# A second-layer triangular solution traced in three parts behind two chunk states, and the gated outputs' store moved from ScalarE's queue to GpSimd's

## The chip, the cores and the metric

The kernel runs on one core of one Trainium2 chip. The core has five engines that work beside each other, each through its own list of instructions and in order: TensorE (PE, matrix products, with its weight load PEld), VectorE (DVE), ScalarE (ACT), GpSimd (POOL) and SyncE (SP, which here only issues DMA transfers). They wait for each other by semaphores. Transfers are issued from the queues of SP, ACT and POOL. The metric is the time of one execution in microseconds (us) on the device.

## The reference

Two residual layers work on 512 tokens of width 2048. The first is differential attention, which the change does not touch. The second is RWKV-7 time mixing: 32 heads of 64 channels carry a matrix state S over the tokens.

```
def step(S, inp):
    r_t, w_t, k_t, v_t, a_t, b_t = inp
    sa = jnp.einsum('bhvk,bhk->bhv', S, a_t)
    S = S * w_t[:, :, None, :] + sa[..., None] * b_t[:, :, None, :] + v_t[..., None] * k_t[:, :, None, :]
    y = jnp.einsum('bhvk,bhk->bhv', S, r_t)
    return S, y
...
y = (y - mean) * lax.rsqrt(var + GN_EPS)            # per head, then gain, bias and a bonus term
y = y.reshape(B, T, RW_WIDTH).astype(h.dtype) * jax.nn.silu(g)
return y @ w_out, v_first
```

r, k, v and the gate g come from one projection of the normalised input, mixed with the token before; w, a and b come from two narrow projections and k.

## The kernel before

**Tiles.** The second layer (`layer1`) goes over 16 pairs of heads (128 channels). The loop variable is j; one pass is called a round here. A pair's 512 tokens are cut into 8 chunks of 64. Within a chunk the recurrence is a triangular system, so that only the state between chunks is sequential.

**A round** runs four projections on PE, `pp` in the profile (L122): v of pair j, k of pair j+1, the gate of pair j-2, r of pair j+1. Each has 16 blocks of 128 rows times three products (high and low halves of fp32 numbers), in two halves. The weights come by SP in 512 KB loads (`wraw`, L78), ACT makes the high half (`wh`, L105), DVE the low half (`wl`, L106), which frees the `wraw` buffer for the next load.

**The chain of a pair** (`t_combine`, `scan_pair`) is threaded between the projection's matmuls one round later: pair j-1 in round j. For each chunk c, PE makes `sm` from the state `VS` and the tile `G` (L1490), ACT copies `rhs` (L1493), PE multiplies by the solution `TT` (L1501), ACT copies the result into `VS` (L1503), PE makes the next state's sum (L1508), and DVE writes the state of chunk c+1 in two halves (L1512, L1515 for the first). "The state of chunk 5" is the one that is written after the step of chunk 4. Between two products stand 6 or 8 projection matmuls. At the end PE makes the outputs `Y` (L1530, L1534), DVE centres them (L1545 to L1547).

**The solution** (`t_solve`) inverts the triangular blocks of pair j in round j, on DVE: 31 steps i, each a product into `tmpl` (L1374) and an addition into `Tm` (L1376). Step i has a row of 31-i columns and i//4+1 blocks, which is how a step is known in the profile (128x66 is step 20). Then comes a multiply (L1377), and SP stores `Tm` into DRAM as `td` (L1378). At the next chain's start SP reads it back in four loads (`TT`, L1391); DVE transposes their first blocks (`T`, L1401, one instruction for each head), PE makes `px` from T and G (L1407), ACT copies it to `X` (L1410), PE makes `px` from TT and X (L1418). In between, the same stretch makes the next pair's Gram products `gp` (L1317), which need `AR` (DVE, L1290). ACT's cast `sHx` of `mixr` (L1112), which is DVE's next product (L1291), stands ahead of the copy X on ACT.

**The gate's output** (`gated`): `mixv` is the gate (`gate`: tanh on ACT, L1455; product on DVE, L1456), times `y` (L1461). ACT's queue stores it into the DRAM tensor yd2 (`yd`, L1464), from where the out projection reads it much later.

**What sets the order.** The program is traced in one order of Python calls; a scheduler then orders each engine's list when the kernel is built, by priority and by its own estimate of when inputs are ready. `high_priority(offset=...)` moves a piece ahead: the projections' splits by 2000 (`AHEAD`), the chain by 3000 (`SCAN`), the solution by 4000 (`SOLVE`). `issue_after(x)` keeps a piece behind instruction x. A chain's step is also allowed to run small pieces (`others`) once a chunk.

Of the kernel before, what the change touches and what calls it, by code (L numbers as in the profile page):

```python
# [18 lines left out]
ALU = mybir.AluOpType  # L19
# [4 lines left out]
P = 128  # L24
D = 2048
# [13 lines left out]
AHEAD, SCAN, SOLVE = 2000, 3000, 4000  # L39


def ahead(offset):


    def deco(f):
        def g_(g, *a, **k):
            with g.tc.high_priority(offset=offset):
                return f(g, *a, **k)

        return g_  # L50

    return deco
# [1055 lines left out]
def split_act(g, src, pool, tag):  # L1108
    nc = g.nc
    hh = pool.tile(list(src.shape), F32R, name="sH" + tag, tag=tag + "H", bufs=1)  # L1110
    hl = pool.tile(list(src.shape), F32R, name="sL" + tag, tag=tag + "L", bufs=1)
    nc.scalar.copy(hh[:], src)  # L1112
    nc.vector.tensor_sub(hl[:], src, hh[:].bitcast(F32))
    return hh, hl
# [35 lines left out]
HALF = 32  # L1150
NG = 4
# [54 lines left out]
LAG = 2  # L1206
# [76 lines left out]
def stage2(g, j, r, p):  # L1283

    nc = g.nc
    while g.later:
        g.later.pop(0)[1]()
    col = lambda n: g.prm[n][:, j : j + 1]
    with g.tc.high_priority(offset=2 * SOLVE if 0 < j <= LAG else 0):
        nc.vector.tensor_mul(p.AR[:, :, 1, :], r[:].rearrange("p (c t) -> p c t", c=NC_), p.E[:, :, 1:])  # L1290
    nc.vector.scalar_tensor_tensor(r[:], r[:], col("hrk"), p.f[:], ALU.mult, ALU.mult)  # L1291
    p.rf = r
# [51 lines left out]
def turn_keys(g, p, c0):  # L1344

    nc = g.nc
    ps = g.ps.tile([P, 512], F32, name="pt", tag="pb", bufs=2)
    for i in range(4):
        nc.tensor.transpose(ps[:, i * P : (i + 1) * P], p.BK[:, c0 + i].rearrange("p s t -> p (s t)"), g.ident[:])
    nc.scalar.copy(p.BKT[:, c0 : c0 + 4], ps[:].rearrange("p (c k) -> p c k", c=4))  # L1350


@ahead(SOLVE)
def t_solve(g, j, p):


    nc, w = g.nc, g.work
    NQ = HALF // NG
    LT = w.tile([P, HALF + 1, HALF], F32, name="LT", tag="LT", bufs=1)
    Tm = w.tile([P, NQ, HALF], F32, name="Tm", tag="Tm", bufs=1)  # L1360
    tmp = w.tile([P, NQ * HALF], F32, name="tmpl", tag="tmpl", bufs=1)
    for i in range(NG):
        ld = nc.gpsimd.dma_start(out=LT[i * 32 : i * 32 + 32], in_=g.ltd[j % 2].rearrange("b h c s t -> (b h c) s t"))
    n2 = LT[:, HALF, :]
    nc.vector.tensor_scalar(n2, n2, 1e-24, None, ALU.max)
    nc.vector.reciprocal(n2, n2)
    nc.gpsimd.memset(Tm[:], 0.0)
    tf = Tm[:].rearrange("p q t -> p (q t)")
    for i in range(NG):
        nc.gpsimd.memset(tf[i * 32 : i * 32 + 32, i :: HALF + NG], 1.0)  # L1370
    for i in range(HALF - 1):
        n, s = HALF - 1 - i, i // NG + 1
        tt = tmp[:, : n * s].rearrange("p (a b) -> p a b", a=s)
        nc.vector.scalar_tensor_tensor(tt, LT[:, i : i + 1, i + 1 :].to_broadcast([P, s, n]), n2[:, i : i + 1],  # L1374
                                       Tm[:, 0:s, i : i + 1].to_broadcast([P, s, n]), ALU.mult, ALU.mult)
        nc.vector.tensor_add(Tm[:, 0:s, i + 1 :], Tm[:, 0:s, i + 1 :], tt)  # L1376
    nc.vector.tensor_mul(Tm[:], Tm[:], n2[:, None, :].to_broadcast([P, NQ, HALF]))  # L1377
    nc.sync.dma_start(out=g.td[j % 2].rearrange("q l t -> l q t"), in_=Tm[:])  # L1378
    return ld.ins


GAP_D, GAP_X, GAP_T = 18, 10, 8


def t_combine(g, j, p, lead):
# [52 lines left out]
def turn_values(g, p):  # L1438

    nc, w, v = g.nc, g.work, p.v  # L1440
    p.VS = w.tile([P, NC_, 2, C], F32, name="VS", tag="VS", bufs=2)
    ps = g.ps.tile([P, 512], F32, name="pt", tag="pd", bufs=1)
    for t in range(NT):
        nc.tensor.transpose(ps[:, t * P : (t + 1) * P], v[:, t * P : (t + 1) * P], g.ident[:])
    pv = ps[:].rearrange("p (t h n) -> p t h n", t=NT, h=2)
    for h in range(2):
        for par in range(2):
            nc.scalar.copy(p.VS[(1 - h) * C : (2 - h) * C, par : NC_ : 2, h, :], pv[par * C : par * C + C, :, h, :])
# [11 lines left out]
def gated(g, j, p, gt, last=False):  # L1460
    g.nc.vector.tensor_mul(gt[:], gt[:], p.y[:])  # L1461
    if last:
        return
    g.nc.scalar.dma_start(out=g.yd2[j * P : (j + 1) * P, :], in_=gt[:])  # L1464


HEADS = ((0, slice(0, C)), (1, slice(C, P)))
# [2 lines left out]
def chain(g, j, p, delay, gap, gap_s, others=(), lead=GAP_D - GAP_T):  # L1470
    def steps():
        yield from t_combine(g, j, p, lead)
        yield from scan_pair(g, j, p, gap, gap_s, dict(others))

    p.chain = Chain(g, steps(), delay)
    return p.chain
# [74 lines left out]
def group_norm(g, j, p):  # L1551
    p.chain.finish(g)
    nc, w, yc = g.nc, g.work, p.yc
    NG = 2 * NT
    sq = w.tile([P, NG, C], F32, name="ysq", tag="ysq", bufs=1)
    nc.scalar.activation(sq[:], yc[:], AF.Square)
    var = g.small.tile([P, NG], F32, name="var", tag="var", bufs=3)
    nc.vector.reduce_sum(var[:], sq[:], AX.X)
    nc.vector.tensor_scalar(var[:], var[:], 1.0 / C, GN_EPS, ALU.mult, ALU.add)
    rs = g.small.tile([P, NG], F32, name="rsg", tag="rsg", bufs=3)  # L1560
    rsqrt(g, rs[:], var[:], NG, "r8")
    nc.vector.tensor_mul(yc[:], yc[:], rs[:, :, None].to_broadcast([P, NG, C]))


def finish_y(g, j, p, bank=("pd", 1)):
    nc, yc = g.nc, p.yc
    ps = g.ps.tile([P, 512], F32, name="pt", tag=bank[0], bufs=bank[1])
    for t in range(NT):
        nc.tensor.transpose(ps[:, t * P : (t + 1) * P], yc[:, 2 * t : 2 * t + 2, :].rearrange("p h n -> p (h n)"),
                            g.ident[:])  # L1570
    nc.vector.scalar_tensor_tensor(p.y[:], ps[:], g.prm["hgw"][:, j : j + 1], p.y[:], ALU.mult, ALU.add)


def layer1(g, aps):
    nc, tc = g.nc, g.tc
    with ExitStack() as cx:
# [6 lines left out]
        def proj(i, j, **k):  # L1583
            return unit_chan(g, (aps["rw_w_in"], i * KT + j), P, **k)[0]
# [17 lines left out]
        for j in range(D // P):  # L1602
            p = pairs[j]
            if j:
                others = [(0, lambda p=p: turn_keys(g, p, 0)), (1, lambda p=p: turn_keys(g, p, 4)),
                          (2, lambda p=p: turn_values(g, p))]
                if j > LAG + 1:
                    others[0] = (0, lambda p=p, i=j - 2: (turn_keys(g, p, 0), finish_y(g, i, pairs[i])))
                elif j > 1:
                    others.append((3, lambda i=j - 2: finish_y(g, i, pairs[i])))  # L1610
                full = LAG < j < D // P - 1
                gaps = ((6, 8) if j > LAG + 1 else (5, 6)) if full else (4, 4) if j > LAG else (4, 5)
                leads = {1: 64, LAG: 18, LAG + 1: 42}
                chain(g, j - 1, pairs[j - 1], 5, *gaps, others, leads.get(j, GAP_D - GAP_T)).step(g)
            stage2(g, j, r, p)
            normed = j > LAG + 1 and pairs[j - 2].chain.wait is None
            if normed:
                group_norm(g, j - 2, pairs[j - 2])

            def behind(m, j=j, p=p, normed=normed):  # L1620
                if j > 1:
                    pairs[j - 2].chain.finish(g)
                with tc.issue_after(m.ins):
                    gram(g, j, p, j > LAG + 1 and pairs[j - 1].chain)
                p.rfs = split_act(g, p.rf[:], w, "x")
                mask_gram(g, p, 0)
                loaded = t_solve(g, j, p)
                with tc.issue_after(loaded):
                    mask_gram(g, p, 1)
                if j > 1 and not normed:  # L1630
                    group_norm(g, j - 2, pairs[j - 2])

            stage_v(g, j, p, proj(2, j, behind=(18, behind)))
            if j == 0:
                turn_keys(g, p, 0)
                turn_keys(g, p, 4)
                turn_values(g, p)
            if j == 1:
                first = gate_of(0, "g0")
            if j + 1 < D // P:  # L1640
                begin(j + 1)
            if j > LAG:
                gated(g, j - LAG, pairs[j - LAG], gate_of(j - LAG))
            if j + 1 < D // P:
                r = receptances(j + 1)
            if j == LAG:
                gated(g, 0, pairs[0], first)
# [52 lines left out]
        for nm in ("11", "21", "22", "12"):  # L1700
            t, c = PLACES[nm]
            a = w.tile([P, 2, 512], F32, name="acc", tag="AR", bufs=3)
# [86 lines left out]
```

## Time and profile before

| | |
|---|---|
| three runs | 2084.47, 2084.9, 2086.21 us (median 2084.9) |
| the profiled execution | 2085.74 us, its span 2084.0 |
| PE busy | 2056.8 us, 99% of the span |
| DVE busy | 1605.5 us, 77% |
| ACT busy | 1124.6 us, 54% |
| POOL busy | 392.4 us, 19% |
| granted TensorE clock | 1.000 |

Names in the profile are `out<-in`, L is the line of the code, x the count. A `q` behind an engine (SPq, ACTq) is its queue issuing a transfer. In a timeline the first number is the start and the second the length in us; what stands in brackets is the idle time of the engine before it and what ended it. Matmul ends are modelled, so the distance between two starts says more about PE than the lengths. The rows of one steady round, shown below from about 1350 to 1421 us, stand for all of rounds 4 to 14.

### The profile page before, as it was taken

Reading aid. Unit: us, or ns where it says so; the run is one execution under the profiler, and the core shown is the slowest. Engines: PE = TensorE matmul, PEld = TensorE weight load, DVE = VectorE, ACT = ScalarE, POOL = GpSimd, SP = SyncE. Lnnn points to the kernel's source line nnn. Section 1 sums busy time; section 2 is a strip of 40 time slices with the busy share of each in tenths; the row PEclk is TensorE's granted clock in tenths of the full one; section 3 lists DMA queues with packets and bytes.
Section 4 is the critical chain, followed back from the end, with each engine's and each line's share of the span. In section 5 each row is a group of like instructions: output and inputs, shape, how many; then the busy total and the mean of one; then the engine's idle time right before and its main releaser. Section 6 shows DMA issues by size and latency. Waiting matters only on the chain.

```text
span 2084.0 us, 34169 instructions
## 1 busy us (share of the span) xinstructions
PE 2056.8 (99%) x11948; PEld 1675.6 (80%) x11948; DVE 1605.5 (77%) x4113; ACT 1124.6 (54%) x2238; POOL 392.4 (19%) x751
## 2 busy tenths in 40 slices
PE   9999999999999999999999999999999999999999
PEld 7888888888888888878777787888888778877887
DVE  6988988888898976475778878777777887767645
ACT  5765656556665544355465555555555555545322
POOL 1020211102011000101222332232332222232001
PEclk9999999999999999999999999999999999999999
DMA  8487978879788966723333332323333233346565
GB/s 271 143 175 192 179 173 184 164 190 166 188 180 169 273 214 172 167 78 111 97 81 92 92 96 85 96 79 100 99 95 90 84 94 91 101 135 189 185 162 121
DMA packets 159549, 294.61 MB, mean 141 GB/s; under 512 B 64416, under 2 KB 81824, under 8 KB 159376
## 3 DMA queue, kind: packets, MB, share of 16 engines
q1 hardware_dynamic: 110912, 184.91, 28.8%
q0 software_dynamic: 23808, 83.54, 22.2%
q10 hardware_dynamic: 24656, 23.97, 3.6%
q8 instruction: 94, 1.54, 0.3%
q14 instruction: 79, 0.65, 0.1%
HBM read 268.71 MB, written 23.66 MB: 140 GB/s over the span
## 4 chain that ended last, share of the span: by engine, by line
PE 75%; DVE 17%; ACT 3%; issue 3%; DMA 2%; ACTq 0%; DVEq 0%; SPq 0%
PE pp L122 35%; PE pp L573 21%; PE pt L122 5%; DVE tmpl L1374 3%; DVE wl L106 3%; DVE Tm L1376 2%; PE gp L1317 1%; PE sc L122 1%; PE sm L1490 1%; ACT wh L105 1%; PE o L122 1%; DVE VS L1512 1%; PE lora L122 1%; PE z L122 1%; PE sm L1501 1%
## 5 line engine op out<-in xcount | busy, mean ns | idle before, releaser
L106 DVE TENSOR_TENSOR wl<-wraw,wh 128x1024 fp32r<-128x1024 f32 (+2 forms) x291 | 356.4, 1225 | 210.8 <-ACT wh L105 202.4
L105 ACT CAST wh<-wraw 128x1024 fp32r<-128x1024 f32 (+2 forms) x291 | 303.6, 1043 | 266.2 <-PE pp L122 133.1
L122 PE MATMUL pp<-hL,wh 128*128 128x512 f32 x1024 | 414.2, 404 | 0.0
L122 PE MATMUL pp<-hH,wh 128*128 128x512 f32 x1024 | 413.2, 404 | 0.0
L122 PE MATMUL pp<-hH,wl 128*128 128x512 f32 x1024 | 412.9, 403 | 0.0
L122 PEld LDWEIGHTS pp<-hH,wh 128*128 128x128 f32 x1024 | 193.2, 189 | 34.5 <-issue 0.2
L122 PEld LDWEIGHTS pp<-hL,wh 128*128 128x128 f32 x1024 | 193.2, 189 | 33.4
L122 PEld LDWEIGHTS pp<-hH,wl 128*128 128x128 f32 x1024 | 193.4, 189 | 32.5
L573 PE MATMUL pp<-wh,hH 128*128 128x512 f32 x448 | 177.0, 395 | 0.0
L573 PE MATMUL pp<-wh,hL 128*128 128x512 f32 x448 | 175.8, 393 | 0.0
L1496 POOL COPY SA<-VS 64x64 f32<-64x64 f32 x224 | 74.4, 332 | 415.9 <-DVE VS L1512 380.1
L122 PE MATMUL pp<-wh,hH 128*128 128x512 f32 x372 | 145.9, 393 | 2.4 <-ACT hH L1103 2.4
L122 PE MATMUL pp<-wh,hL 128*128 128x512 f32 x372 | 146.5, 394 | 0.1
L122 PE MATMUL pp<-wl,hH 128*128 128x512 f32 x372 | 145.9, 392 | 0.5 <-DVE wl L106 0.5
L1374 DVE SCALAR_TENSOR_TENSOR tmpl<-LT,Tm 128x60 f32<-128x60 f32 (+24 forms) x496 | 134.0, 270 | 12.3
L573 PE MATMUL pp<-wl,hH 128*128 128x512 f32 x448 | 140.4, 392 | 0.0
L1376 DVE TENSOR_TENSOR Tm<-Tm,tmpl 128x60 f32<-128x60 f32 (+24 forms) x496 | 104.2, 210 | 11.9
L1493 ACT COPY rhs<-sm 64x64 f32<-64x64 f32 x256 | 52.8, 206 | 105.9 <-PE sm L1490 86.1
L573 PEld LDWEIGHTS pp<-wl,hH 128*128 128x128 f32 x448 | 84.5, 189 | 17.2
L573 PEld LDWEIGHTS pp<-wh,hH 128*128 128x128 f32 x448 | 84.2, 188 | 17.3 <-issue 0.3
L573 PEld LDWEIGHTS pp<-wh,hL 128*128 128x128 f32 x448 | 84.3, 188 | 16.1
L1503 ACT COPY VS<-sm 64x64 f32<-64x64 f32 x256 | 52.7, 206 | 77.9 <-PE sm L1501 70.3
(400 smaller groups left out, 4367.4 us busy)
## 6 DMA issues: line engine op xcount, KB each, us to landing
wraw<-in_rw_w_in_dram SPq DMA_DIRECT2D x128, 512.0 KB
wraw<-in_da_w_in_dram SPq DMA_DIRECT2D x75, 512.0 KB
wraw<-in_da_w_in_dram POOLq DMA_DIRECT2D x28, 512.0 KB, 6.5
wraw<-in_da_w_out_dram SPq DMA_DIRECT2D x26, 512.0 KB
wraw<-in_rw_w_out_dram SPq DMA_DIRECT2D x26, 512.0 KB
Ta<-in_da_w_in_dram POOLq DMA_DIRECT2D x21, 512.0 KB, 5.8
Tb<-in_da_w_in_dram POOLq DMA_DIRECT2D x21, 512.0 KB, 5.8
Tc<-in_da_w_in_dram POOLq DMA_DIRECT2D x21, 512.0 KB, 5.8
```

What stands on the lines that cost most here:

```text
L105: a = nc.scalar.copy(hi[:, ks], raw[:, ks])
L106: d = nc.vector.tensor_sub(lo[:, ks], raw[:, ks], hi[:, ks].bitcast(F32))
L122: m = nc.tensor.matmul(out, a, b, start=s, stop=e, skip_group_check=skip)
L573: m = nc.tensor.matmul(out[t][:], x, wt[lo][:, k, :], start=first, stop=end and lo == 1 and k == KG - 1, skip_group_check=True)
L1317: m = nc.tensor.matmul(gp[h][:, i * P : (i + 1) * P], BK[r_, c0 + i, :, :], p.AR[r_, c0 + i, :, :], start=True, stop=True)
L1374: nc.vector.scalar_tensor_tensor(tt, LT[:, i : i + 1, i + 1 :].to_broadcast([P, s, n]), n2[:, i : i + 1], Tm[:, 0:s, i : i + 1].to_broadca ...
L1376: nc.vector.tensor_add(Tm[:, 0:s, i + 1 :], Tm[:, 0:s, i + 1 :], tt)
L1490: nc.tensor.matmul(sm[:, 0:P], both(p.G[:, c, 0]), both(VS[:, c]), start=True, stop=True)
L1493: nc.scalar.copy(rhs[r_, :], sm[r_, h * C : h * C + C])
L1496: nc.gpsimd.tensor_copy(p.SA[r_, c - 1, :], VS[r_, c, h, :])
L1501: nc.tensor.matmul(sm[:, P : P + C], both(g.TT[j % 2][:, c]), rhs[:], start=True, stop=True)
L1503: g.copied = nc.scalar.copy(VS[r_, c, h, :], sm[r_, P : P + C])
```

## The change

The solution's steps become a generator in three parts: steps 0 to 20, 21 to 28, and 29 to 30 with the multiply and the store `td`. In rounds 3 to 14 (`full`) the first part is traced where the whole was; the second is traced by the chain of the pair before, in its step of chunk 4, behind the instruction that writes the state of chunk 5, and the third in its step of chunk 6, behind the state of chunk 7. In the other rounds the solution stays in one piece. Apart from that, `gated` issues its store from POOL's queue instead of ACT's. No instruction is added or removed; 14 stores change queues.

```
-    for i in range(HALF - 1):
-        ...
-    nc.vector.tensor_mul(Tm[:], Tm[:], n2[:, None, :].to_broadcast([P, NQ, HALF]))
-    nc.sync.dma_start(out=g.td[j % 2].rearrange("q l t -> l q t"), in_=Tm[:])
+    def steps(a, b):
+        for i in range(a, b):
+            ...
+    def parts():
+        for a, b in zip(PARTS, PARTS[1:]):
+            with g.tc.high_priority(offset=SOLVE), g.tc.issue_after(g.state.ins) if a and split else ExitStack():
+                steps(a, b)
+                if b == HALF - 1:
+                    nc.vector.tensor_mul(Tm[:], Tm[:], n2[:, None, :].to_broadcast([P, NQ, HALF]))
+                    nc.sync.dma_start(out=g.td[j % 2].rearrange("q l t -> l q t"), in_=Tm[:])
+            if split:
+                yield
+    p.solve = parts()
+    next(p.solve, None)
...
+PARTS = 0, 21, 29, HALF - 1
...
-    g.nc.scalar.dma_start(out=g.yd2[j * P : (j + 1) * P, :], in_=gt[:])
+    g.nc.gpsimd.dma_start(out=g.yd2[j * P : (j + 1) * P, :], in_=gt[:])
...
+                if full:
+                    others += [(c, lambda p=p: next(p.solve)) for c in (4, 6)]
...
-                loaded = t_solve(g, j, p)
+                loaded = t_solve(g, j, p, LAG < j < D // P - 1)
```

The order of the lists moves as follows (in the changed kernel lines behind the edit have numbers 14 higher, L1512 is L1526, and L1374, L1376, L1377 and L1378 are L1376, L1378, L1385 and L1386).

DVE around the state of chunk 5 (`VS`), before:

```order
L1374 SCALAR_TENSOR_TENSOR tmpl<-LT,Tm 128x66
L1376 TENSOR_TENSOR Tm<-Tm,tmpl 128x6x11
L1374 SCALAR_TENSOR_TENSOR tmpl<-LT,Tm 128x60
L1376 TENSOR_TENSOR Tm<-Tm,tmpl 128x6x10
L1374 SCALAR_TENSOR_TENSOR tmpl<-LT,Tm 128x54
L1512 SCALAR_TENSOR_TENSOR VS<-sm,gam,Sg 64x64
```

and in the changed kernel:

```order
L1376 SCALAR_TENSOR_TENSOR tmpl<-LT,Tm 128x66
L1378 TENSOR_TENSOR Tm<-Tm,tmpl 128x6x11
L1526 SCALAR_TENSOR_TENSOR VS<-sm,gam,Sg 64x64 x2
L1376 SCALAR_TENSOR_TENSOR tmpl<-LT,Tm 128x60
L1263 TENSOR_TENSOR f<-f,mixk 128x512
```

The state's two halves stand three rows of the solution earlier, right behind step 20.

DVE around the state of chunk 7, before (mixv is the gate, sLup a split of two narrow weights that SP loads into a `wraw` buffer):

```order
L1374 SCALAR_TENSOR_TENSOR tmpl<-LT,Tm 128x16
L1144 SCALAR_TENSOR_TENSOR mixv<-pp,mu,mixv 128x511
L1376 TENSOR_TENSOR Tm<-Tm,tmpl 128x8x2
L1374 SCALAR_TENSOR_TENSOR tmpl<-LT,Tm 128x8
L1376 TENSOR_TENSOR Tm<-Tm,tmpl 128x8
L1377 TENSOR_TENSOR Tm<-Tm,LT 128x256
L1512 SCALAR_TENSOR_TENSOR VS<-sm,gam,Sg 64x64 x2
L1456 SCALAR_TENSOR_TENSOR mixv<-thg,mixv 128x512
L1461 TENSOR_TENSOR mixv<-mixv,y 128x512
L1113 TENSOR_TENSOR sLup<-upw,sHup 96x256
L106 TENSOR_TENSOR wl<-wraw,wh 128x1024
```

and in the changed kernel:

```order
L1470 SCALAR_TENSOR_TENSOR mixv<-thg,mixv 128x512
L1526 SCALAR_TENSOR_TENSOR VS<-sm,gam,Sg 64x64 x2
L1376 SCALAR_TENSOR_TENSOR tmpl<-LT,Tm 128x16
L1475 TENSOR_TENSOR mixv<-mixv,y 128x512
L1378 TENSOR_TENSOR Tm<-Tm,tmpl 128x8x2
L1113 TENSOR_TENSOR sLup<-upw,sHup 96x256
L1376 SCALAR_TENSOR_TENSOR tmpl<-LT,Tm 128x8
L1378 TENSOR_TENSOR Tm<-Tm,tmpl 128x8
L1385 TENSOR_TENSOR Tm<-Tm,LT 128x256
L106 TENSOR_TENSOR wl<-wraw,wh 128x1024
```

The last two steps and the multiply went behind the state and are mixed with the gate's second product and the split; the gate's first product went ahead of the state.

SP from the narrow weights (`upw`) on, before:

```order
L1589 DMA upw<-in_rw_decay_up_dram 96x128
L1590 DMA upw<-in_rw_iclr_up_dram 96x128
L1378 DMA td<-Tm 128x8x32
L78 DMA wraw<-in_rw_w_in_dram 128x1024
L1391 DMA TT_9512<-td 32x8x32 x4
L78 DMA wraw<-in_rw_w_in_dram 128x1024 x2
```

and in the changed kernel:

```order
L1603 DMA upw<-in_rw_decay_up_dram 96x128
L1604 DMA upw<-in_rw_iclr_up_dram 96x128
L78 DMA wraw<-in_rw_w_in_dram 128x1024
L1386 DMA td<-Tm 128x8x32
L78 DMA wraw<-in_rw_w_in_dram 128x1024
L1405 DMA TT_9512<-td 32x8x32 x4
L78 DMA wraw<-in_rw_w_in_dram 128x1024
```

One load of weights went ahead of td, so that td and TT each stand behind one now. The same holds from round 4 to round 13; round 14 has weights only between td and TT. On DVE the second transpose T (L1401) went three to five rows behind the first, among small operations of the group norm, and two of those went behind the split that follows. PE's list keeps its order but for a few places in rounds 3 and 4, ACT's steady rounds lose only the store, and on POOL the store stands behind the last copy of a chain's state, ahead of memsets.

More of the change, by code (lines that the diff above doesn't have):

```diff
@@ L1353, in t_solve @@
 @ahead(SOLVE)
-def t_solve(g, j, p):
+def t_solve(g, j, p, split):
     nc, w = g.nc, g.work
@@ L1370, in t_solve @@
         nc.gpsimd.memset(tf[i * 32 : i * 32 + 32, i :: HALF + NG], 1.0)
-    for i in range(HALF - 1):
[L1372 to L1378, printed above, removed]
+    def steps(a, b):
+        for i in range(a, b):
+            n, s = HALF - 1 - i, i // NG + 1
+            tt = tmp[:, : n * s].rearrange("p (a b) -> p a b", a=s)
+            nc.vector.scalar_tensor_tensor(tt, LT[:, i : i + 1, i + 1 :].to_broadcast([P, s, n]), n2[:, i : i + 1],
+                                           Tm[:, 0:s, i : i + 1].to_broadcast([P, s, n]), ALU.mult, ALU.mult)
+            nc.vector.tensor_add(Tm[:, 0:s, i + 1 :], Tm[:, 0:s, i + 1 :], tt)
+    def parts():
[9 more added lines that the diff above has]
+    next(p.solve, None)
     return ld.ins
 GAP_D, GAP_X, GAP_T = 18, 10, 8
+PARTS = 0, 21, 29, HALF - 1
 def t_combine(g, j, p, lead):
```

## The prediction

> **What bounds it now.** I read three views: the windows of one round of the second layer (a pass of the pair loop; rounds 4 to 14 are alike), the waits of TensorE (PE) over those rounds, and the timeline of one round.
>
> ```profile
> 1208.00:1268.30 60.30, 59.59 (x428) 48.65 (x427) 46.70 (x131) 32.90 (x75) 16.93 (x37) 1.00 0.32 94
> ```
>
> The columns are the stretch, its length, the busy time of PE, its weight loads, DVE, ACT and POOL, the granted clock, DMA share and GB/s. PE is busy for 59.59 of 60.30 us at full clock. So a round can only win back PE's few stops. Over rounds 4 to 14 (1208 to 1850 us) these are all of PE's waits (total us, times, longest):
>
> ```profile
> core 0 of [0], span 2084.0 us
> PE sm L1490 <- DVE VS L1512: 4.6, 12, 0.4
> PE sm L1501 <- ACT rhs L1493: 3.6, 11, 0.3
> ```
>
> Two waits, about once a round each. The timeline of PE in one round prices them:
>
> ```profile
> 1392.82 0.39 PE L122 MATMUL pp<-hL,wh 128*128 128x512 f32 x1
> 1393.05 0.39 PE L122 MATMUL pp<-hH,wl 128*128 128x512 f32 x1
> 1393.81 0.46 PE L1490 MATMUL sm<-VS,G 128*128 128x128 f32 x2 [0.38 <-DVE VS L1512]
> ...
> 1404.71 0.42 PE L1490 MATMUL sm<-VS,G 128*128 128x128 f32 x2
> ...
> 1406.13 0.40 PE L122 MATMUL pp<-hH,wh 128*128 128x512 f32 x1
> 1406.85 0.43 PE L1501 MATMUL sm<-rhs,TT 128*128 128x64 f32 x2 [0.33 <-ACT rhs L1493]
> ```
>
> A projection matmul gives way to the next after 0.23 us (1392.82 to 1393.05). The product on the state of chunk 5 starts 0.76 us after its forerunner: 0.53 lost. The one on rhs of chunk 7 starts 0.72 us after: 0.49 lost. Both together, 1.02 us a round, are what this change can win there. Now who causes them, on DVE and ACT:
>
> ```profile
> 1392.95 0.27 DVE L1512 SCALAR_TENSOR_TENSOR VS<-sm,gam,Sg 64x64 f32<-64x64 f32 x1
> ...
> 1403.12 0.23 DVE L1374 SCALAR_TENSOR_TENSOR tmpl<-LT,Tm 128x8 f32<-128x8 f32 x1
> 1403.38 0.17 DVE L1376 TENSOR_TENSOR Tm<-Tm,tmpl 128x8 f32<-128x8 f32 x1
> 1403.59 0.43 DVE L1377 TENSOR_TENSOR Tm<-Tm,LT 128x256 f32<-128x256 f32 x1
> 1403.93 0.60 DVE L1512 SCALAR_TENSOR_TENSOR VS<-sm,gam,Sg 64x64 f32<-64x64 f32 x2
> 1404.56 0.69 DVE L1456 SCALAR_TENSOR_TENSOR mixv<-thg,mixv 128x512 f32<-128x512 f32 x1
> 1405.28 0.69 DVE L1461 TENSOR_TENSOR mixv<-mixv,y 128x512 f32<-128x512 f32 x1
> 1405.89 0.41 DVE L1113 TENSOR_TENSOR sLup<-upw,sHup 96x256 fp32r<-96x256 f32 x1
> ```
>
> ```profile
> 1404.50 0.41 ACT L1112 CAST sHup<-upw 96x256 fp32r<-96x256 f32 x1 [0.75 <-DMA upw<-in_rw_iclr_up_dram]
> 1406.01 0.33 ACTq L1464 DMA_DIRECT2D yd<-mixv  x1
> 1406.38 0.42 ACT L1493 COPY rhs<-sm 64x64 f32<-64x64 f32 x2 [1.46 <-DVE sLup L1113]
> ```
>
> The state of chunk 5 is written behind steps of the solution. The rhs copy stands on ACT behind the issue of the store, which waits for the gated product of DVE (1405.28, done at 1405.97).
>
> **The change, part by part.** *Chunk 5.* Three rows of the solution leave the front of the state; the step in the rows above takes 0.47 us from start to start (1403.12 to 1403.59), so one and a half are about 0.7. The state moves from 1392.95 to 1392.2. The product began 0.86 us after the state's first half (1392.95 to 1393.81), so it could begin at 1393.1, before its turn at 1393.28: 0.53 won.
>
> *Chunk 7.* Two steps (0.94) and the final multiply (0.34 until the state begins) leave its front; the gate's product L1456 (0.69) enters it. The state moves forward 0.6, to 1403.3; its product, at 0.78 behind the state (1403.93 to 1404.71), can start at 1404.1, and its turn is now 1404.18. No new stop, with 0.1 to spare.
>
> *The store.* ACT no longer waits for the gated product, so rhs follows sHup (1404.91) and the product on chunk 7: 0.49 won. Fourteen issues of 0.33 leave ACT, which was not the bound. POOL takes them; behind each stand there only memsets and, late in the next round, a copy. Its issue has no row for a store, but four issues by POOL took 2.02:
>
> ```profile
> 1366.05 2.02 POOL L1363 DMA_DIRECT2D LT<-ltd  x4 [2.40 <-DMA ltd<-G]
> ```
>
> So 0.5 each, hidden by POOL's idle time. The data (256 KB) moves about 1 us earlier, since the gated product now comes right behind the state of chunk 7.
>
> *What is late next: the solution's way through DRAM.* Behind the state of chunk 7 now come, in this order, a half step, L1461, another half, sLup, a step and the multiply: 0.60 + 0.94 + 0.69 + 0.41 + 0.43, about 3.0 from 1403.3. td is issued at about 1406.3 instead of 1404.08. SP's queue also changes places: the weights that wait for sLup go ahead of td (at about 1405.4), and the next weights, freed by the split behind the multiply (about 1407.3), ahead of the four TT loads. What such neighbours do, two other places show:
>
> ```profile
> 1404.08 0.39 SPq L1378 DMA_DIRECT2D td<-Tm  x1
> 1406.33 0.35 SPq L78 DMA_DIRECT2D wraw<-in_rw_w_in_dram  x1
> 1406.77 1.99 SPq L1391 DMA_DIRECT2D TT<-td  x4
> ```
>
> ```profile
> 1824.98 0.33 SPq L78 DMA_DIRECT2D wraw<-in_rw_w_in_dram  x1
> 1825.55 0.32 SPq L461 DMA_DIRECT2D yr<-yd  x1
> 1826.97 0.37 SPq L1378 DMA_DIRECT2D td<-Tm  x1
> 1830.50 1.80 SPq L1391 DMA_DIRECT2D TT<-td  x4
> ```
>
> ```profile
> 1009.95 2.17 DMA td<-Tm
> ```
>
> ```profile
> 1889.87 0.33 SPq L78 DMA_DIRECT2D wraw<-in_rw_w_out_dram  x1
> 1892.70 1.80 SPq L1391 DMA_DIRECT2D TT<-td  x4
> ```
>
> ```profile
> 1894.80 0.44 DVE L1401 STREAM_TRANSPOSE T<-TT 64x256 f32<-64x256 f32 x1 [0.46 <-DMA TT<-td]
> ```
>
> td alone lands in 2.17 (chain, at 1009.95). Behind weights and a 256 KB row it took 3.53 (1826.97 to 1830.50), and its readers were issued 5.52 after the weights. Here the 256 KB are the store, on another queue but at the same time: TT at 1405.4 + 5.5 = 1410.9 at worst, at 1406.3 + 2.2 = 1408.5 at best. I take 1410.7, nearer the former, as the same sizes are moved. The first TT then needs 2.10 (1892.70 to 1894.80, where DVE waited for it, weights ahead): T at 1412.8. What hangs on T, in the stretch where the next round begins:
>
> ```profile
> 1412.20 0.90 DVE L1401 STREAM_TRANSPOSE T<-TT 64x256 f32<-64x256 f32 x2
> ...
> 1416.87 0.69 DVE L1290 TENSOR_TENSOR AR<-mixr,E 128x512 f32<-128x512 f32 x1
> ```
>
> ```profile
> 1418.86 2.06 PE L1317 MATMUL gp<-AR,BK 64*128 64x128 f32 x32
> 1420.85 0.34 PE L1418 MATMUL px<-TT,X 32*32 32x32 f32 x9
> ```
>
> ```profile
> 1419.29 0.74 ACT L1410 COPY X<-px 32x256 f32<-32x256 f32 x2
> ```
>
> DVE runs in order, so AR, the product behind it, ACT's cast of that and then X all hang on T. With T at 1412.20, X was done at 1420.03, 7.83 later; the second transpose and two small operations now trade places, which saves about 0.35: 7.5. T at 1412.8 gives X at 1420.3. PE, 1.02 ahead, wants it at 1420.85 - 1.02 = 1419.83: about 0.55 lost with 0.1 for the semaphore. gp is in time (AR at 1412.8 + 5.0 = 1417.8, wanted 1417.84).
>
> *Sum.* Won 11 x 1.02 = 11.2; lost 0.55 in the ten rounds (4 to 13) whose order has weights on both sides of td: 5.5. Round 14 has no weights ahead of td: nothing lost. The first split round (3) has other waits: taken as nothing. Net -5.7 us on a span of 2084.0. The profiled execution took 2085.74, 0.04% above the median of 2084.9; I lower the median by 5.4, to 2079.5.
>
> A rule bears on this. The Trainium skill ("DMA: Bandwidth & Descriptors", Queues, rings and completion order) says that each DMA engine takes the descriptors of one queue in ring order. By it td and TT stand behind both weights and the sum is the one above; were it not so, the loads would be in time and the sum -11.2. The slow td at 1826.97 bears it out.
>
> **The rivals.** *The loads are hidden anyway.* td needs 2.2, TT is issued at 1408.5 and T is ready at 1410.6, before DVE gets there at 1411.2 (1412.20 - 1.02). For it speaks that T never waited in the steady rounds. Net -11.2: 2073.5.
>
> *Slower: POOL's store gets between.* It decides from T at 1413.3: then X at 1420.8 costs PE the whole 1.02. A store 1.1 us later than I put it would move its 256 KB onto td, and T to 1413.9: 1.65 lost, +0.6 a round in ten rounds, -1.0 in one: 2090. For it speaks how long POOL can be held beside DVE:
>
> ```profile
> 1399.32 1.32 POOL L1496 COPY SA<-VS 64x64 f32<-64x64 f32 x1 [0.32 <-DVE VS L1512]
> ```
>
> ```profile
> L1496 POOL COPY SA<-VS 64x64 f32<-64x64 f32 x224 | 74.4, 332 | 415.9 <-DVE VS L1512 380.1
> ```
>
> Beside a DVE product this copy took 1.32 instead of its mean of 0.33, and sLup and the multiply run on DVE just when the store is issued; against it, the four issues at 1366.05 kept their 0.5 each. The Trainium skill ("SBUF — State Buffer", SBUF: two separate sides) warns of just this: a DMA from POOL's queue starves while DVE holds the port that the two share. No row here shows a held POOL store.
>
> *The split saves nothing at chunk 5.* DVE has the same work, so the stop moves to chunk 7, where only 0.1 is spare: were L1456 held by its tanh for 0.6, all of the 0.53 returns. Then -0.49 + 0.55 a round: 2085.5, no change.
>
> **Chances.** Forecast 0.45 (its own range 2075.5 to 2084), hidden loads 0.20, POOL's store 0.20, nothing at chunk 5 0.15. The 8 in 10 range runs from 2073 to 2091, which takes in both ends of T. A change under 0.2% (4.2 us) can't be told from none here: faster than 2080.7 are the hidden loads and 0.26 of the forecast, 0.46; within are 0.18 of the forecast and 0.12 of the last, 0.30; slower 0.24.
>
> **What would show it.** The wait for VS in PE's list shrinks to a few, the one for rhs disappears; yd is issued by POOL near 1405; td 2.2 us later in its round; T's transposes gain an idle time that ends on the TT load, and PE waits for X at L1418. I am wrong if T waits over 2 us, or not at all, or if chunk 7 has taken over the wait.

## The result and the profile after

| | before | changed |
|---|---|---|
| runs | 22, median 2086.93 us | 22, median 2092.66 us (2089.71 to 2098.51) |
| profiled execution, its span | 2085.74, 2084.0 us | 2092.51, 2090.8 us |
| PE, DVE, ACT, POOL busy | 2056.8, 1605.5, 1124.6, 392.4 us | 2055.3, 1604.2, 1123.8, 386.8 us |

The change makes the kernel slower: the ratio is 1.0027, 95% interval 1.0021 to 1.0034. The work is the same, and the span is 6.8 us longer. "Y" is from here on the start of a round's first output product (L1530, L1544), and "5.8 behind Y" means so many us after it. The windows of the ten steady rounds, from Y to Y (stretch, length, then busy time of PE, PEld, DVE, ACT, POOL, the clock, DMA share, GB/s), before:

```profile
1227.72:1831.55 603.83, 596.30 (x4262) 486.58 (x4261) 467.31 (x1290) 328.70 (x749) 168.09 (x370) 1.00 0.33 94
```

and after:

```profile
1227.86:1834.81 606.95, 594.67 (x4262) 486.93 (x4261) 465.10 (x1289) 327.69 (x749) 163.13 (x380) 1.00 0.32 94
```

They lose 3.1 us at the same clock. The period before them loses 0.8, and the two behind them 2.2 and 1.4 (from the starts of the Y products). PE's waits over the second layer's rounds (total us, times, longest):

```profile
core 0 of [0], span 2090.8 us
PE px L1432 <- ACT X L1424: 7.0, 11, 0.7
PE gp L1317 <- DVE AR L1290: 6.0, 8, 1.6
PE sm L1515 <- ACT rhs L1507: 0.3, 1, 0.3
```

The wait for VS is gone from the list and the one for rhs all but gone; two others are there. Their cause stands in DVE's list of waits:

```profile
DVE T L1415 <- DMA TT<-td: 24.0, 11, 3.0
```

T, which did not wait in the steady rounds before, now waits 2.2 us a round in the mean. One round's timeline shows how that spreads. SP and POOL ahead of Y (1409.37):

```profile
1407.18 0.35 SPq L78 DMA_DIRECT2D wraw<-in_rw_w_in_dram  x1
1408.04 0.39 SPq L1386 DMA_DIRECT2D td<-Tm  x1
1409.24 0.33 SPq L78 DMA_DIRECT2D wraw<-in_rw_w_in_dram  x1
1412.77 1.82 SPq L1405 DMA_DIRECT2D TT<-td  x4
```

```profile
1407.37 0.62 POOL L1478 DMA_DIRECT2D yd<-mixv  x1 [1.19 <-DVE tmpl L1376]
```

DVE:

```profile
1415.38 0.44 DVE L1415 STREAM_TRANSPOSE T<-TT 64x256 f32<-64x256 f32 x1 [2.39 <-DMA TT<-td]
...
1417.03 0.44 DVE L1415 STREAM_TRANSPOSE T<-TT 64x256 f32<-64x256 f32 x1
...
1417.59 1.22 DVE L106 TENSOR_TENSOR wl<-wraw,wh 128x1024 fp32r<-128x1024 f32 x1
1418.72 0.74 DVE L1144 SCALAR_TENSOR_TENSOR mixr<-pp,mu,mixr 128x511 f32<-128x511 f32 x1
...
1419.50 1.06 DVE L1290 TENSOR_TENSOR AR<-mixr,E 128x512 f32<-128x512 f32 x1
...
1420.98 0.74 DVE L1291 SCALAR_TENSOR_TENSOR mixr<-mixr,prm_hrk,f 128x512 f32<-128x512 f32 x1
```

ACT and PE:

```profile
1421.75 0.62 ACT L1112 CAST sHx<-mixr 128x512 fp32r<-128x512 f32 x1 [5.59 <-DVE mixr L1291]
1422.28 0.26 ACT L1304 COPY ssl<-pt 128x128 f32<-128x128 f32 x1
1422.56 0.74 ACT L1424 COPY X<-px 32x256 f32<-32x256 f32 x2
```

```profile
1418.59 0.69 PE L1421 MATMUL px<-T,G 32*32 32x32 f32 x32
...
1420.62 2.06 PE L1317 MATMUL gp<-AR,BK 64*128 64x128 f32 x32 [0.98 <-DVE AR L1290]
1423.35 0.69 PE L1432 MATMUL px<-TT,X 32*32 32x32 f32 x32 [0.68 <-ACT X L1424]
```

X's own input, px of L1421, is done at 1419.28, and ACT has nothing else to do: X waits 3.3 us for its place behind sHx. T itself is in time for PE, which has no wait at L1421 here.

### The profile page after: what moved, and what is told of

It reads as the page before. It is cut to its first block, busy times and chain, and to the rows that moved or that the text cites. A ratio compares the mean times of both kernels' runs of the same rounds, so it can differ in the third digit from the quotient of the medians.

```text
span 2090.8 us, 34199 instructions
## 1 busy us (share of the span) xinstructions
PE 2055.3 (98%) x11948; PEld 1675.5 (80%) x11948; DVE 1604.2 (77%) x4113; ACT 1123.8 (54%) x2238; POOL 386.8 (18%) x765
## 4 chain that ended last, share of the span: by engine, by line
PE 70%; DVE 17%; DMA 5%; ACT 4%; issue 3%; ACTq 0%; SPq 0%; DVEq 0%
PE pp L122 31%; PE pp L573 22%; PE pt L122 5%; DVE wl L106 4%; DMA td<-Tm 3%; DVE tmpl L1376 2%; DMA TT<-td 2%; DVE Tm L1378 1%; PE sc L122 1%; PE o L122 1%; DVE VS L1526 1%; PE sm L1504 1%; PE lora L122 1%; PE z L122 1%; PE sm L1522 1%
## 5 line engine op out<-in xcount | busy, mean ns | idle before, releaser
L1376 DVE SCALAR_TENSOR_TENSOR tmpl<-LT,Tm 128x60 f32<-128x60 f32 (+24 forms) x496 | 134.2, 270 | 12.8
L1510 POOL COPY SA<-VS 64x64 f32<-64x64 f32 x224 | 57.3, 256 | 420.3 <-DVE VS L1526 383.5
L1378 DVE TENSOR_TENSOR Tm<-Tm,tmpl 128x60 f32<-128x60 f32 (+24 forms) x496 | 104.0, 210 | 11.1
```

What stands on the lines that cost most here:

```text
L1510: nc.gpsimd.tensor_copy(p.SA[r_, c - 1, :], VS[r_, c, h, :])
```

## The experiments

**How they are read.** For each kernel the table gives the median, then what PE loses in a round at four places: the distance from the start of a product's forerunner to its own start, less 0.23 us for the chunk products (the distance of two projection matmuls) and less the kernel before's distance for gp and px (mean of nine rounds, the ten without their first). Then come, from the timelines, means of ten rounds: td's issue against Y, the time from there to the issue of the first TT load, which waits for td, and T's start behind Y. The kernels under one "before" were timed beside it, and a time is best compared with that one. In experiments 1 and 5 to 8 the time came 1.3 to 3.0 us below the range of the theory that held, and why is not shown; the waits are what they were to tell.

| kernel | us | VS | rhs | AR | X | td | td to TT | T |
|---|---|---|---|---|---|---|---|---|
| before | 2086.93 | 0.75 | 0.49 | 0 | 0 | -4.58 | 2.69 | 3.54 |
| changed | 2092.66 | 0.31 | 0.02 | 0.61 | 0.69 | -1.32 | 4.92 | 5.80 |
| *before, beside 1 to 4* | 2085.76 | | | | | | | |
| 1 store only | 2078.87 | 0.72 | 0.00 | 0.04 | 0.08 | -3.99 | 2.70 | 3.64 |
| 2 split only | 2084.05 | 0.28 | 0.00 | 0.53 | 0 | -1.38 | 4.26 | 5.62 |
| 3 two parts | 2090.77 | 0.66 | 0.01 | 0.53 | 0.48 | -2.30 | 3.40 | 5.56 |
| 4 td by ACT | 2091.58 | 0.32 | 0.01 | 0.55 | 0.74 | -1.36 | 4.91 | 5.78 |
| *before, beside 5 to 8* | 2086.33 | | | | | | | |
| 5 X first | 2082.73 | 0.28 | 0.00 | 0.56 | 0 | -1.31 | 4.88 | 5.81 |
| 6 X and AR first | 2075.03 | 0.29 | 0.05 | 0.04 | 0 | -1.31 | 4.89 | 5.85 |
| 7 split, AR first | 2075.83 | 0.27 | 0.00 | 0.00 | 0 | -1.38 | 4.17 | 5.71 |
| 8 old solution | 2073.44 | 0.27 | 0.00 | 0.00 | 0 | -1.32 | | 3.54 |
| *before, beside 9 to 12* | 2085.78 | | | | | | | |
| 9 before, both orders | 2085.87 | 0.71 | 0.50 | 0 | 0 | -4.58 | 2.69 | 3.54 |
| 10 store, both orders | 2079.64 | 0.69 | 0.00 | 0.00 | 0 | -3.99 | 2.71 | 3.64 |
| 11 td ahead | 2079.53 | 0.29 | 0.00 | 0.33 | 0 | -1.33 | 2.73 | 6.18 |
| 12 all | 2074.76 | 0.26 | 0.06 | 0.08 | 0 | -1.32 | 2.70 | 5.95 |
| *before, beside 13 to 15* | 2085.26 | | | | | | | |
| 13 second weights behind | 2085.85 | 0.28 | 0.02 | 0.22 | 0.63 | -1.31 | 4.88 | 5.43 |
| 14 TT by ACT | 2097.71 | 0.35 | 0.01 | 0.97 | 0.54 | -1.06 | 2.73 | 6.34 |
| 15 weights behind TT | 2075.98 | 0.28 | 0.00 | 0.00 | 0 | -1.32 | 2.65 | 3.64 |

**1 to 4: which part, and by which way.** Two theories stood against each other. Q: the solution's late store td, behind a load of weights on SP's queue, costs the time. S: POOL's 256 KB get between.

Experiment 1 is the kernel before with the store alone:

```
-    g.nc.scalar.dma_start(out=g.yd2[...], in_=gt[:])
+    g.nc.gpsimd.dma_start(out=g.yd2[...], in_=gt[:])
```

> The kernel before with one line of the change, the gated store issued by POOL; the triangular solution is left in one part. Theory Q (the loss comes from the third part of the solution, which issues td some 3 us later against Y, behind a load of weights on SP's queue): nothing of that is here, so the rhs stop goes (0.49 us in each of 11 rounds) and the time is 2081 to 2083 beside 2086.9 for the kernel before; the T transpose doesn't wait. Theory S (the loss comes from POOL's store, whose 256 KB land between the weights and td): the store lands in this kernel too, about when the TT loads do, so T waits and the time is 2086 or more.

It is faster than before (0.9972, 0.9962 to 0.9982). The rhs stop is gone and T is nearly always in time.

Experiment 2 is the changed kernel with that line as before (store by ACT), so the split alone:

> The changed kernel with the gated store issued by ACT as before; only the split is left. Theory Q: td is as late as in the changed kernel, T waits some 2 us in each round, and the rhs stop of 0.49 us per round is back: 2095 to 2099 (2092.7 and about 5). Theory S: without the store's packets td lands in 2.2 us as before, not in 4.7, T waits under 0.3 us, the waits for X and AR go (some 1.2 us a round), the rhs stop is back: 2082 to 2086.

The time is S's, but not for its reason: T comes 5.62 behind Y, nearly as late as in the changed kernel, with no store on POOL; yet the kernel is no slower than before (0.9993, 0.9983 to 1.0003). So T's lateness has no fixed price. The experiment does not take the 256 KB away: they go by ACT's queue, 2.65 ahead of Y instead of 2.30. From td to TT it takes 0.66 less so (4.26), but T comes only 0.18 sooner. The rhs stop is gone here too, since the split lets the gate's products come ahead: either part alone wins it.

Experiment 3 holds nothing behind the state of chunk 7:

```
-PARTS = 0, 21, 29, HALF - 1
+PARTS = 0, 21, HALF - 1
-    others += [(c, lambda p=p: next(p.solve)) for c in (4, 6)]
+    others += [(c, lambda p=p: next(p.solve)) for c in (4,)]
```

> The changed kernel with two parts in place of three: steps 21 to 30 stand behind the state of chunk 5, and nothing is held behind the state of chunk 7. On SP's queue td then stands ahead of both loads of weights, and on DVE the multiply by n2 comes some 1.2 us earlier than in the changed kernel. Theory Q: td lands in 2.2 to 3 us, T waits under 0.7 us a round, the gain at chunk 5 and at rhs stays (about 1 us a round), a part of the stop at chunk 7 is back: 2077 to 2082. Theory S: the store still lands there, td takes over 4 us, T waits over 1 us: 2086 to 2091.

Slower than before (1.0025, 1.0014 to 1.0035). Neither theory fits: the time and T's wait are S's, but from td to TT it takes 3.40, between the two. td is issued 1 us earlier and ahead of both loads of weights, but T comes only 0.24 earlier. The stop has moved to chunk 7: its product loses 0.51 us a round there (0.22 in the changed kernel).

Experiment 4 takes td off SP's queue:

```
-    nc.sync.dma_start(out=g.td[j % 2]..., in_=Tm[:])
+    (nc.scalar if split else nc.sync).dma_start(out=g.td[j % 2]..., in_=Tm[:])
```

> The changed kernel with td issued by ACT's queue in the rounds with the split (the TT loads stay on SP's). Theory Q in its narrow form (the ring: td waits behind the weights on SP's queue): from td's issue to TT's falls from 4.7 us to under 3.2, T is 1.5 us earlier, and the time is 2079 to 2084, if ACT's wait for the multiply holds nothing that PE wants. Theory S, or lines shared by all queues: td takes 4 us or more on any queue, 2091 to 2094.

From td's issue to TT's it takes 4.91 us, on SP's queue 4.92. Another queue wins nothing; 2091.58.

**5 to 8: what makes a late T cost.** The split alone and the changed kernel have nearly the same late T; what differs most is ACT's order: with the split alone the scheduler has put the copy X ahead of the cast sHx, otherwise behind it. That gives a new theory (Q2): T's wait holds everything behind it on DVE, so AR is late for gp, and mixr for sHx; X is late only because it stands behind sHx.

Experiment 5 turns this one order round in the changed kernel:

```
+    g.x = nc.scalar.copy(X[hi], ...)
...
+    with tc.issue_after(g.x.ins) if j > LAG + 1 else ExitStack():
         p.rfs = split_act(g, p.rf[:], w, "x")
```

> The changed kernel with one order turned round: on ACT the cast sHx (L1112) is issued behind the copy X (L1424), not ahead of it. Nothing else moves on PE or DVE. Theory Q2 (T's wait holds DVE; AR and the mixr of L1291, which stand behind T there, come late; X is late because it stands behind sHx on ACT, and sHx needs that mixr): px's wait for X, 0.69 us a round over before, goes; gp's wait for AR, 0.61 us a round, stays; 2084 to 2086. Rival P (as predicted: X is late because px L1421 gets T late): px waits for X as long as before, 2091 to 2094.

X's wait is gone (0.69 to 0), AR's is not (0.56). (The rival there is put more simply than the prediction had it, which knew the way by AR and the cast.) ACT in one of its rounds:

```profile
1417.52 0.74 ACT L1424 COPY X<-px 32x256 f32<-32x256 f32 x2 [3.19 <-PE px L1421]
...
1419.30 0.62 ACT L1112 CAST sHx<-mixr 128x512 fp32r<-128x512 f32 x1 [0.75 <-DVE mixr L1291]
```

X now follows px, 1.8 us ahead of the cast.

Experiment 6 also puts the variance and its rsqrt (nine rows) behind AR on DVE:

```
+    g.ar = nc.vector.tensor_mul(p.AR[:, :, 1, :], ...)
...
+    with tc.issue_after(g.ar.ins):
         group_norm(g, j - 2, pairs[j - 2])
```

> The changed kernel with both orders turned round: X ahead of sHx on ACT, and on DVE the variance and its rsqrt (L1572 to L1576, nine rows between and behind the two T transposes) behind AR (L1290). T waits as long as in the changed kernel, but some 1.2 us of DVE's work behind it is out of AR's way. Theory Q2: gp's wait for AR falls from 0.61 to under 0.2 us a round, X's is gone: 2078 to 2082. Rival R (AR is late for what POOL's copy or the store does to DVE, not for its place behind T): gp still waits 0.5 us, 2084 to 2086.

It takes 2075.03 us and beats both kernels (0.9951 to before, 0.9938 to 0.9963). DVE's and PE's waits of this kernel:

```profile
DVE T L1415 <- DMA TT<-td: 29.0, 21, 3.0
```

```profile
PE gp L1317 <- DVE AR L1290: 0.2, 1, 0.2
```

T waits even more than in the changed kernel (29.0 us against 24.0), and PE loses 0.2 us in all.

Experiment 7 does the same to the split alone:

> The split alone (store by ACT, where X already stands ahead of sHx), with the variance and its rsqrt behind AR on DVE. The split alone took 2084.05 and waited 0.53 us a round more for AR than before. Theory Q2: that wait falls under 0.15 us, 2078 to 2081, level with the store alone. Rival R: as the split alone, 2083 to 2085.

AR's wait is gone in the nine rounds of the table (0.53 to 0.00); in the first of the ten, where T came 7.33 behind Y, gp still lost 1.05. The time is 2075.83 us.

Experiment 8 leaves the orders and gives T its data in time. Its TT loads read the td of the round before, so it computes with an old solution:

```
-    in_=g.td[j % 2]...
+    in_=g.td[(j + (LAG < j < D // P - 1)) % 2]...
```

> The changed kernel with only T's data in time: in the rounds with the split the four TT loads read the td slot of the round before (the solution used is an old one), so they don't wait for this round's td. The third part of the solution, td, the POOL store and the order on ACT (X behind sHx) stay as they are. Theory Q2: T doesn't wait, AR and the mixr of L1291 come as early as before, X's and AR's waits both go although X stands behind sHx; 2076 to 2080 (the gains at chunk 5 and rhs, 0.9 us a round, are left). Rival R or S (the store on POOL or DVE's contention costs the time): at least 0.5 us a round of these waits stays, 2084 or more.

T does not wait, X stands behind sHx as in the changed kernel, and all new waits are gone: 2073.44. Q2 holds: the changed kernel's loss is T's wait, passed on by two orders.

**9 to 12: controls, and td ahead.** Experiment 9 turns both orders round in the kernel before, experiment 10 in the one with the store alone.

> The kernel before, without any part of the change, with the two orders turned round (X ahead of sHx on ACT; the variance and its rsqrt behind AR on DVE). A control. Theory Q2 (the orders only cure the lateness that a late T brings): PE waits for neither X nor AR in the kernel before, so nothing is won: 2085 to 2088 beside 2086.3. Rival O (the orders are a gain by themselves, whatever T does): 2076 to 2080.

2085.87 beside 2085.78: the orders win nothing by themselves.

> The store by POOL alone, unsplit, with the two orders turned round. Theory Q2: T is in time there, so the orders win only the 0.12 us a round that X and AR cost it in some rounds: 2077 to 2079; the version with the split as well (2075.0) stays below it by the stop at chunk 5, 0.4 to 0.5 us a round, 3 to 5 us in all. Rival O: as fast as the version with the split, 2074 to 2076, so that the split is worth nothing.

2079.64, no better than the store alone. So the split is worth about 5 us once its side effect is cured: experiment 6 is 11.3 below its before, experiment 10 is 6.1 below its own. That is about what the split wins at the chunk products: 0.40 a round (0.69 to 0.29), 4.4 in eleven rounds.

Experiment 11 is the changed kernel with the first load of weights held behind td; the lines are in `load_w`, with a count that finds that load:

```
+    with g.tc.issue_after(held) if held else ExitStack():
         ld = (queue or g.nc.sync).dma_start(out=raw[:, ks.start : ks.stop], ...)
```

> The changed kernel with the first of the two loads of weights held behind td on SP's queue; the scheduler then puts X ahead of sHx by itself, so it is compared with the changed kernel with X first (2082.7, from td's issue to TT's 4.9 us). Theory W (td is slow for the 512 KB that are in flight ahead of it, on whatever queue): from td to TT falls to 3.0 to 3.6 us as in the kernel with two parts, T comes at 4.3 to 4.7 us behind Y, and gp's wait for AR falls from 0.55 to under 0.25 us a round: 2077 to 2080. Rival S (POOL's 256 KB are what is in the way): still over 4.3 us, 2082 to 2084.

The time is as expected, the reason is not: td lands in 2.73 us, with POOL's store there as before, but T comes at 6.18. One of its rounds:

```profile
1405.56 0.39 SPq L1392 DMA_DIRECT2D td<-Tm  x1
1406.05 1.21 SPq L84 DMA_DIRECT2D wraw<-in_rw_w_in_dram  x2
1408.28 2.45 SPq L1412 DMA_DIRECT2D TT<-td  x4
```

```profile
1413.31 0.44 DVE L1422 STREAM_TRANSPOSE T<-TT 64x256 f32<-64x256 f32 x1 [1.41 <-DMA TT<-td]
```

The weights went behind td and in front of TT: what td won, TT lost (5.0 us from issue to T). The gain against the changed kernel goes with the lists on ACT and DVE, which the scheduler made anew: X stands ahead of sHx, so that its wait is gone, and one wl stands ahead of T's second half, where from T to AR's end it takes 4.25 us in most rounds, against 4.82. These lists were not tested apart from the move of td.

Experiment 12 adds both orders to that.

> The changed kernel with both orders turned round and td ahead of the first weights. Theory Q2: with the orders turned a T that is 1 to 2 us late costs nothing any more, so an earlier td wins under 0.1 us a round: 2074 to 2076, level with both orders alone (2075.0). Rival: T's lateness still costs DVE's later work, 2071 to 2073.

2074.76 (0.9947, 0.9933 to 0.996), level with experiment 6.

**13 to 15: what pins T.** T came 5.6 to 6.2 behind Y in every version with the split (but for 8, which does not wait for td), whichever way td went. Experiment 13 holds only the second load of weights behind TT, 14 issues the TT loads by ACT's queue with td ahead as in 11, 15 holds both loads behind TT (13 and 15 by the lines of 11, with `held` set to the last TT load and another count).

> The changed kernel with one order of SP's queue turned round: the second load of weights (issued 0.1 us ahead of Y's start) is held behind the four TT loads; the first stays ahead of td; X stays behind sHx. Theory B (T is pinned by the second weights, which share the lines with td or stand ahead of TT): T comes at 4.4 to 5.0 us behind Y in place of 5.8, the waits for X and AR fall from 1.3 to under 0.7 us a round, 2081 to 2086. Rival A (the first weights and the store are what holds td): from td to TT stays 4.9, T at 5.6 or later, 2091 to 2094.

T comes 0.37 earlier, less than expected, and td still takes 4.88: the first weights hold it. 2085.85, since X's wait stays.

> The changed kernel with td ahead of both loads of weights and the four TT loads issued by ACT's queue (ACT is idle there); both loads of weights stay where they are on SP's. Theory B in its form by rings (TT waits behind the weights on SP's queue): td lands in 2.7, TT is issued at 1.4 to 2 us behind Y and T comes 2.1 to 2.7 later, at 3.6 to 4.5 us, where SP's TT loads gave 6.2 with td just as early: 2074 to 2079. By shared lines (any queue's data waits for the 1 MB of weights): T at 5.3 or later, 2083 to 2092.

TT on a queue of its own comes no sooner:

```profile
1410.64 1.82 ACTq L1412 DMA_DIRECT2D TT<-td  x4
```

```profile
1416.11 0.44 DVE L1422 STREAM_TRANSPOSE T<-TT 64x256 f32<-64x256 f32 x1 [3.20 <-DMA TT<-td]
```

It takes 5.5 us from issue to T, with the loads of weights issued on SP from 1408.45 on. In one of the ten rounds td came 2.7 us later than in the others; without it T's mean is 6.13. The time, 2097.71, is worse than either form of the theory gave, and why stays open. PE's waits are only 1.6 us longer in all than in the changed kernel; two of the profiled rounds ran at a granted clock of 0.95 and took 64 us.

> The changed kernel with both loads of weights held behind the TT loads on SP's queue: td and TT have queue and lines to themselves but for the store. Both forms of theory B: td lands in 2.7, T comes at 3.5 to 4.1 us behind Y, the waits for X and AR go, 2074 to 2079, if the weights, now 5 us later, still come in time. Rival S (POOL's 256 KB): T still at 5 or later. If the weights come too late, PE waits for wh or wl instead, 2085 or more.

```profile
1401.76 0.39 SPq L1392 DMA_DIRECT2D td<-Tm  x1
1404.44 2.35 SPq L1411 DMA_DIRECT2D TT<-td  x4
1406.95 3.96 SPq L84 DMA_DIRECT2D wraw<-in_rw_w_in_dram  x3
```

```profile
1401.10 0.63 POOL L1485 DMA_DIRECT2D yd<-mixv  x1 [1.19 <-DVE tmpl L1382]
```

```profile
1406.62 0.43 DVE L1422 STREAM_TRANSPOSE T<-TT 64x256 f32<-64x256 f32 x1
```

With POOL's store issued 0.7 us ahead of td and no weights in the way, T is in time (3.64 behind Y, 3.54 is DVE's own pace), X stays behind sHx, and PE loses nothing to AR and X in these ten rounds: 2075.98 (0.9951, 0.9936 to 0.9966). So the 1 MB of weights holds the solution's way through DRAM, on whichever queue it goes; POOL's store alone does not. The windows of the traces agree: in the changed kernel's round above, the 16 DMA engines were at a share of 0.9 or more from 1409 to 1413, while td was on its way. Beside the weights the store has a part in td's time: with it on ACT (experiments 2 and 7) from td to TT took 4.26 and 4.17, with it on POOL (the changed kernel and 6) 4.92 and 4.89, but T came only 0.1 to 0.2 sooner.

## Why the prediction was wrong

Forecast 2079.5, measured 2092.66: slower where faster was forecast. Of the 13.2 us between them 2.0 are the base, since the kernel before took 2086.93 beside it, not 2084.9. The change cost 5.7 us where 5.4 were to be won. By the prediction's own steps:

- *Chunk 5*: right. The product on its state started 0.776 us after its forerunner, now 0.230: 0.55 won, 0.53 forecast. Chunks 4 and 6 win another 0.11.
- *Chunk 7*: wrong by 0.22. "No new stop, with 0.1 to spare" was a loss of 0.22 a round (0.233 to 0.450). The state was to be written 0.88 ahead of its product's turn (1403.3 against 1404.18) and came 0.50 ahead (1405.22 against 1405.72). Part of that is the tanh, which the last rival named: the gate's product waited 0.11 for it in each round. The rest stays open.

```profile
1403.95 0.63 ACT L1469 ACTIVATE thg<-mixv 128x512 f32<-128x512 f32 x1 [0.28 <-DVE mixv L1144]
```

```profile
1404.61 0.69 DVE L1470 SCALAR_TENSOR_TENSOR mixv<-thg,mixv 128x512 f32<-128x512 f32 x1
1405.22 0.59 DVE L1526 SCALAR_TENSOR_TENSOR VS<-sm,gam,Sg 64x64 f32<-64x64 f32 x2
```

- *The store*: right, 0.47 of 0.49 a round. POOL began it 0.30 us behind the gated product's end (0.64 in one round), where ACT had needed 0.03, and its issue took 0.62, not 0.5; PE waited for nothing behind it. But the split wins the same stop (experiment 2), so the two gains don't add up if one is left out.
- *What is late next*: the mechanism was right, with T, AR, the cast and X in one line, and td at the forecast place: 1.34 ahead of Y by the forecast, 1.32 measured. This is the step that failed, in its size. From td to TT 4.4 was taken and 4.92 came, and the first TT load to T took 2.20 for 2.10; even the worst case of the prediction, TT 5.5 behind the first weights, was short of the 5.78 measured. T was 5.80 behind Y, not 5.16 (1412.8 less Y at 1408.66 - 1.02). With that, "gp is in time (AR at 1417.8, wanted 1417.84)", a margin of 0.04, became a wait of 0.61, and X's 0.55 became 0.69 on top: 1.30 a round. What hangs on T was sized well: to AR's end it took 4.82 in most rounds (5.0 in the prediction), 5.2 beside POOL's copy, and to X's end 7.55 (7.5), 7.9 beside the copy. With T at 5.80 the prediction's own sum loses 0.55 + 0.64 = 1.19. (Its 0.1 for the semaphore has no row there; from X's end to px it is 0.05 in the rows above.) The prediction named T at 1413.3 (5.66 behind Y) as the point from which the change loses; the measured mean is 0.14 beyond it. A mean hid something too: T ran from 5.20 to 6.65 over the rounds, and lateness costs while earliness pays nothing.
- *Sum*: the ten rounds, forecast at -4.7, gave +3.1. "Round 14 has no weights ahead of td: nothing lost" and "round 3: taken as nothing" failed too: the former lost 0.98 at gp and 0.75 at X by PE's timeline (2.2 in its period, where -1.0 was counted), the latter 0.8. In round 14 it took 2.56 from td to TT, but TT, behind weights as in experiment 11, took 4.85 from its issue to T. The last period's 1.4, where px waits 1.8 for T of the unsplit last solution, swings from kernel to kernel (0.3 less than before to 1.4 more, and 2.8 once, at a granted clock of 0.97); its cause stays open.
- *The rule*. The prediction explained its slow td by ring order (the Trainium skill, "DMA: Bandwidth & Descriptors", Queues, rings and completion order: an engine takes the descriptors of a ring in order), so that td and TT stand behind the weights of their own queue. Experiments 4 and 14 took them off it and nothing came sooner. Another section of the same page of the Trainium skill (Issuing engines are not separate DMA queues) says that transfers of all issuing engines run on the same 16 DMA engines and that several issuers save only issue time: the runs agree with that, 4.91 against 4.92 us from td to TT.
- *The rivals*. The loads were not hidden. "POOL's store gets between" ended on the right side (2090), for the wrong reason: with the store back on ACT's queue T is late all the same (experiment 2), and with it on POOL T can be in time (15). "The split saves nothing at chunk 5" does not hold for the changed kernel; it is what happens with two parts (3).

## What to carry to other kernels

A piece that is moved later on an in-order engine is paid for where its result comes back, so give a sum's smallest margin (here 0.04 us) the error of its largest estimate and forecast over the spread, not at the mean. When a small, urgent transfer is late, look at the bytes that were issued shortly before it, on all queues: holding the bulk loads back won about 15 us here (from 5.7 above its before to 9.3 below), and changing the queue of td or TT won none. And read what stands behind a waiting instruction: a wait of 2 us a round cost 1.3, 0.6 or nothing, by the order of two lists.

## What was not expected of the hardware

- A 512 KB load slows a transfer behind it just as much from another queue: td took 2.7 us with the load issued 0.5 us behind it, and 4.9 with the load issued 0.8 to 0.9 us ahead, on the same queue or not.
- The copy G on POOL (L1428) and AR on DVE disturb each other: AR took 1.06 us in the row of 1419.50 above, where the copy had begun 0.1 ahead of it, and 0.69 in the kernel before, where the copy began after AR was done. In the eleven rounds of the changed kernel AR took 1.06 to 1.10 in the four where the copy began first; in the other seven it took 0.69. POOL's row of the changed kernel:

```profile
1419.41 1.62 POOL L1428 COPY G<-AR 64x512 f32<-64x512 f32 x2 [5.64 <-PE px L1421]
```
